# Gate projections of the convolution layer all last, with value pages held in the gate array until then

## Chip, core and metric

One core of a Trainium2 chip runs one launch of the kernel. The time is device microseconds from the launch's first to its last work; the figure given for a kernel is the median of several runs. A separate execution of each kernel is recorded by the hardware profiler.

## What is computed

One step of a two-layer decoder trunk, on a prompt of 1024 positions and on 8 samples of one position each, with shared weights (model width 1024). Layer 0 has stick-breaking attention heads beside causal pooling groups; the samples attend over a paged cache of 4096 past positions. Layer 1 is a convolution module with a gate:

```python
def c_mix(x, conv_prev, w_in, w_dw, b_dw, cn_g, cn_b, w_out):
    p = x @ w_in
    a, a_gate, gate = jnp.split(p, [CONV_WIDTH, 2 * CONV_WIDTH], axis=-1)
    h = a * jax.nn.sigmoid(a_gate)
    h_ext = jnp.concatenate([conv_prev.astype(h.dtype), h], axis=1)
    c = lax.conv_general_dilated(h_ext, w_dw[:, None, :], ..., feature_group_count=CONV_WIDTH)
    c = jax.nn.silu(layer_norm(c + b_dw, cn_g, cn_b))
    return (c * jax.nn.silu(gate)) @ w_out, h_ext[:, -CONV_STATE:]
```

For the samples, layer 0 needs `o = w . v_past`: 8 samples x 32 pages of 128 positions x 512 values, fetched through `page_table`. Those 256 pages of 256 KB are the value pages of this document.

## The kernel before

**The stretch that matters** is the input projection of layer 1 with the convolution, from some 600 us to 970 us of the span. The generator `c_gen` puts out the projection in 48 *slots*. A slot is one block of 128 output features times one half (512 positions) of the prompt: 8 values of k, three matmuls each (high x high, low x high, high x low parts of the split operands, L225 to L227), so 24 matmuls into one of two accumulators `acc`, then an evacuation by ScalarE. Blocks come in the order of the list `blocks`: `ag0, a0, ag1, a1, ...`; `GATE_AFTER = (3,)` puts the first gate block `g0` behind `a3`, and `g1` to `g7` stand behind `a7`. The last two blocks are interleaved, so that the half 0 of `g6` and `g7` precedes the half 1 of either. I write a3/1 for half 1 of block a3.

- `evac_ag` writes the sigmoid of the gate of channel block cb, `evac_a` copies the block and multiplies (GpSimd) into `HBUF[cb]`, of which there are two buffers. Before a new one is written, the block cb - 2 must be through: `evac_a` first puts out all its remaining taps, and the buffer is free once its last tap (VectorE) and `tail_rows` (a TensorE transposition, put out four points after the join) have read it.
- `conv(cb)` puts the 31 taps of the depthwise convolution of one channel block in two lists: `heads` (ScalarE product L1372, GpSimd addition L1375) and `taps` (VectorE, L1383 and L1385, and a closing addition `join`, L1390). `cpoint`, called four times a slot, pops 1.575 heads and 1.46 taps from them.
- `tick(n)` advances the sample work in `queue` by n steps: first `decode_v`, then `sample_path`. A step of `decode_v` loads four value pages (`v_tile` gives the buffers, a ring of `VB = 9`) and multiplies each with four 32-column matmuls side by side (L1163). The main loop gives `VRATE = 1.575` steps a slot, and 2.7 when only `sample_path` is left.
- When the taps of block 7 are through, the statistics are summed (L1422), and `stats_3` queues the normalization `midq`: broadcast rows by transposition (`mid_a`, L1569), subtract and scale (`mid_b`, VectorE, L1581), SiLU (`mid_s`, ScalarE, L1595); `cpoint` pops one entry per call. After the loop, `mid_g` multiplies with the gate, `mid_c` splits the product for the output projection (`out_layer`, L1034 to L1036).
- `G`, the gate array of 32 KB per partition, is written first by `evac_gate(0)`. TensorE, ScalarE, VectorE and GpSimd run in the order in which the code puts instructions out. The order on SyncE, which issues all loads and stores here, is chosen by the framework's planner from its own estimate of when each is ready.

Of the kernel before, what the change touches and what calls it, by code (L numbers as in the profile page):

```python
# [41 lines left out]
NTB = S // P  # L42
# [35 lines left out]
VB = 9  # L78
# [9 lines left out]
FAST = (5, 7)  # L88
WCONVA = ((0, 5), (1, 5))
SY = 2  # L90
VRATE = 1.575
MOM7 = 3
TAPR = 1.46
SHIFT_LAG = 6
MOM_LAG = 6
GATE_AFTER = (3,)
QSCALE = 1.0 / math.sqrt(DH)


# [1 line left out]
def kernel(  # L101
# [33 lines left out]
    def psum(tag, bufs, shape=(P, 512), dt=F32):  # L135
        return (psq[0] if tag == "qv" else ps).tile(list(shape), dt, tag=tag, name=tag, bufs=bufs)
# [9 lines left out]
    def trp():  # L146
        return pz[0].tile([P, 512], F32, tag="zt", name="zt", bufs=NZT[0])
# [203 lines left out]
    def page_ids(b, j, n):  # L351
        _, pg = nc.values_load_multi_w_load_instructions(
            pt[0:1, b * NPG + j:b * NPG + j + n], engines=[SP], min_val=0, max_val=NPOOL - 1,
            skip_runtime_bounds_check_because="page ids index the page pool")
        return pg
# [113 lines left out]
    queue = []  # L469

    def tick(n):
        while n > 0 and queue:
            try:
                next(queue[0])
                n -= 1
            except StopIteration:
                queue.pop(0)
# [414 lines left out]
    t = trp()  # L892
# [54 lines left out]
    for u in range(len(units) + 2):  # L947
# [10 lines left out]
        k = int(tcred)  # L958
# [171 lines left out]
    def fin0(tb, y, h):  # L1130
        sp.dma_start(x1_dram[tb * P:(tb + 1) * P, h], y[:, h])

        def f():
            for hf in range(h.start // 512, h.stop // 512):
# [10 lines left out]
    load_res(1)  # L1145
    out_layer(w_out0, first0, ahead0, X, [gb0], lnp, fin0,
              lambda n4, tb: tick(1), before0, None, tail0, OLAGB, FASTB, WIDE, gps0)
    def v_tile():
        return cd.tile([P, HW], F32, tag="vt", name="vt", bufs=VB)

    def decode_v():
        for hf in range(2):
            Z = W[hf]
            pv = psum("qv", 1)
            for j in range(NPG):
                if j % 2 == 0:
                    pgs = [page_ids(hf * 4 + bi, j, 2) for bi in range(4)]
                vts = []
                for bi in range(4):
                    vts.append(v_tile())  # L1160
                    sp.dma_start(vts[bi], cv[ds(pgs[bi][j % 2], 1)].rearrange("o t f -> t (o f)"))
                for bi in range(4):
                    pe.matmul(pv[32 * bi:32 * bi + 32, :], Z[:, j % 8 * 4 + j // 8, :], vts[bi],  # L1163
                              start=(j == 0), stop=(j == NPG - 1), tile_position=(0, 32 * bi))
                yield
            m = cx.tile([P, HW], F32, tag="pvm", name="pvm", bufs=2)
            act.activation(out=m, in_=pv, func=AF.Copy)
            mh = m.rearrange("p (h d) -> p h d", d=DH)
            gp.tensor_tensor(out=mh, in0=mh, in1=dmask, op=ALU.mult)
            for _ in range(2):  # L1170
                yield
            t = trp()
            for i in range(4):
                pe.matmul(t[:, i * 4:i * 4 + 4], m[:, i * P:(i + 1) * P], selb, start=True, stop=True)
            sh = shs[:, 0:4, hf * 4:hf * 4 + 4]
            act.activation(out=sh, in_=t[:, 0:16].rearrange("p (k b) -> p k b", b=4), func=AF.Copy)
            gp.tensor_tensor(out=sh, in0=sh, in1=sga[:, :, hf * 4:hf * 4 + 4], op=ALU.mult)
# [7 lines left out]
    def issue():  # L1185
        if rows:
            w, f0, k = rows.pop(0)
            ts = []
            for hf in range(2):
                ts.append(v_tile())  # L1190
                sp.dma_start(ts[hf], w[k * P:(k + 1) * P, f0 + hf * HW:f0 + hf * HW + HW])
            issued.append(ts)
# [143 lines left out]
    def evac_a(cb):  # L1336
        def f(c, c0, n, o):
            if c == 0:
                while any(t[0] <= cb - 2 for t in heads):
                    heads.pop(0)[1]()  # L1340
                while any(t[0] <= cb - 2 for t in taps):
                    pop_tap()
                HBUF[cb] = cx.tile([P, KS + S], F32, tag="hbuf", name="hbuf", bufs=2)
                gp.memset(HBUF[cb][:, 0:KS], 0.0)
            hs = HBUF[cb][:, KS + c0:KS + c0 + n]
            act.activation(out=hs, in_=o, func=AF.Copy)
            gp.tensor_tensor(out=hs, in0=hs, in1=CSG[cb][:, c0:c0 + n], op=ALU.mult)
            if c == 1:
                conv(cb)
        return f  # L1350
# [97 lines left out]
    def cpoint():  # L1448
        credit[1] = min(credit[1] + HRATE, 3.0)
        while credit[1] >= 1.0:  # L1450
            credit[1] -= 1.0
            if heads:
                heads.pop(0)[1]()
        credit[0] = min(credit[0] + TAPR, 3.0)
        while credit[0] >= 1.0:
            credit[0] -= 1.0
            if taps:
                pop_tap()
        midpop()

    def evac_gate(g):
        def f(c, c0, n, o):
            act.activation(out=G[:, c0 // P:(c0 + n) // P, g, :], in_=o.rearrange("p (t c) -> p t c", c=P), func=AF.Silu)
        return f

# [2 lines left out]
    def gate_block(g):  # L1468
        blocks.append((w_in1, 2048 + g * P, evac_gate(g), f"g{g}"))

    gn = 0
    for i in range(NK):
        blocks.append((w_in1, 1024 + i * P, evac_ag(i), f"ag{i}"))
        blocks.append((w_in1, i * P, evac_a(i), f"a{i}"))
        if i in GATE_AFTER:
            gate_block(gn)
# [17 lines left out]
    cd = cdp.enter_context(tc.tile_pool(name="cd", bufs=1, reuse_waits="tile"))  # L1494
    C = cd.tile([P, NTB, NK, P], F32, name="conv")
    G = cd.tile([P, NTB, NK, P], F32, name="gate")
    ones32 = cd.tile([P, 32], F32, name="ones32")
    gp.memset(ones32, 1.0)
    onesm = cd.tile([P, P], F32, name="onesm")
# [17 lines left out]
    stats = psum("o", 1)  # L1517

    queue.append(decode_v())
    queue.append(sample_path())  # L1520
    rmu = const.tile([P, 2, 4], F32, name="rmu")
# [75 lines left out]
    def mid_g(c):  # L1597
# [3 lines left out]
        for tb in range(a, b):  # L1601
            (dve if tb in GDVE else gp).tensor_tensor(out=C[:, tb], in0=C[:, tb], in1=G[:, tb], op=ALU.mult)

# [11 lines left out]
    def before(n4, tb):  # L1615
# [8 lines left out]
        if tb == 3:  # L1624
            gb1[0] = G[:, 0:2].rearrange("p t k c -> p t (k c)")
            sp.dma_start(gb1[0][:, 0, :], ln_c_g.to_broadcast([P, D]))
# [7 lines left out]
    vcred = 0.0  # L1634
    while (f"g{NK - 1}", 0) not in fill.seen:
        for i in range(3):
            fill.part()
            cpoint()
        fill.part()
        vcred += VRATE if len(queue) > 1 else 2.7  # L1640
        tick(int(vcred))
        vcred -= int(vcred)
        cpoint()
# [59 lines left out]
```

## Time and profile before

| | us |
|---|---|
| median of 3 runs | 1110.16 (1109.91 to 1115.74) |
| the profiled execution, whole | 1110.31 |
| its span, first to last instruction | 1108.5 |
| TensorE busy / VectorE busy | 1042.0 / 833.3 |
| mean granted TensorE clock | 0.972 |

The profile has a page (busy shares, the span in slices, the costliest groups) and answers questions on the trace: busy time by stretch, instructions of one engine in order of time with what ended the idle time before each, and waits by pair. In the rows of an engine in order of time the first column is the start, the second the duration of the group, both in us; `x8` is the number of instructions in the group, and a bracket gives the idle time before it and what ended that.

### The profile page before, as it was taken

The numbers are of one execution on the slowest core, as the hardware profiler recorded it, in microseconds if no ns is written. First come the engines' busy times: TensorE is split into PE (matmuls) and PEld (weight loads), VectorE is DVE, ScalarE is ACT, GpSimd is POOL, SyncE is SP. The second block draws the span as 40 slices with busy tenths as digits, with TensorE's granted clock in tenths as the row PEclk, the third lists the DMA queues.
The fourth block names the chain that finished last, engine by engine and source line by source line (L and its number), as shares of the span: only waits on it lengthen the run. The fifth ranks groups of instructions, "written<-read, shape, count | busy, mean of one in ns | idle before, by whom it ended". The sixth has DMA issues, their size and how long they took to land.

```text
span 1108.5 us, 19858 instructions
## 1 busy us (share of the span) xinstructions
PE 1042.0 (94%) x6804; PEld 840.1 (76%) x6804; DVE 833.3 (75%) x982; ACT 493.4 (45%) x933; POOL 632.2 (57%) x488
## 2 busy tenths in 40 slices
PE   8899998999999989979988999999999899799996
PEld 7897887888888878979986666566666466678786
DVE  3368899899689988698874699999999960584246
ACT  5245665665766647601143244534543412462111
POOL 3266858567276878568765266757764612342135
PEclk9999999999999989989988999999999999889998
DMA  8577857865457776478425786877687678386933
GB/s 268 171 205 228 253 181 214 257 207 176 131 158 230 243 217 217 151 263 267 155 100 177 218 262 214 267 241 232 208 263 235 205 244 266 111 271 217 321 108 135
DMA packets 179350, 235.20 MB, mean 212 GB/s; under 512 B 15434, under 2 KB 95955, under 8 KB 179225
## 3 DMA queue, kind: packets, MB, share of 16 engines
q1 hardware_dynamic: 179249, 233.94, 67.0%
q8 instruction: 53, 0.87, 0.3%
q14 instruction: 48, 0.39, 0.1%
HBM read 212.60 MB, written 16.14 MB: 206 GB/s over the span
## 4 chain that ended last, share of the span: by engine, by line
PE 51%; POOL 7%; DVE 6%; DMA 5%; issue 2%; ACT 2%; SPq 2%; POOLq 0%; DVEq 0%; ACTq 0%
PE acc L225 10%; PE acc L227 9%; PE acc L226 9%; PE qv L1163 6%; DMA kt<-in_cache_k_dram 3%; POOL kt L417 2%; PE acc L1034 2%; PE acc L1036 2%; PE acc L1035 2%; DVE conv L1581 2%; PE zt L1034 1%; POOL wlo L210 1%; DVE xl L196 1%; PE qv L1199 1%; PE zt L1035 1%
## 5 line engine op out<-in xcount | busy, mean ns | idle before, releaser
L225 PE MATMUL acc<-xh,whi 128*128 128x384 f32 (+2 forms) x960 | 360.3, 375 | 1.9 <-DVE hbt L705 1.4
L227 PE MATMUL acc<-xl,whi 128*128 128x384 f32 (+2 forms) x960 | 339.3, 353 | 0.5 <-DVE xl L196 0.5
L226 PE MATMUL acc<-xh,wlo 128*128 128x384 f32 (+2 forms) x960 | 338.8, 353 | 0.0
L417 POOL TENSOR_TENSOR kt<-kt,qbs 128x1024 f32<-128x1024 f32 x96 | 237.8, 2487 | 79.0 <-DMA kt<-in_cache_k_dram 58.8
L210 POOL TENSOR_TENSOR wlo<-wraw,whi 128x512 fp32r<-128x512 f32 x122 | 163.6, 1345 | 176.6 <-ACT whi L205 154.0
L1385 DVE SCALAR_TENSOR_TENSOR conv_acc<-hbuf,wdwT,conv_acc 128x1024 f32<-128x1024 f32 x196 | 252.8, 1290 | 6.8
L225 PEld LDWEIGHTS acc<-xh,whi 128*128 128x128 f32 x960 | 183.0, 191 | 68.5 <-issue 27.2
L227 PEld LDWEIGHTS acc<-xl,whi 128*128 128x128 f32 x960 | 182.8, 190 | 18.4 <-DVE xl L196 0.9
L226 PEld LDWEIGHTS acc<-xh,wlo 128*128 128x128 f32 x960 | 183.4, 191 | 15.8
L409 DVE TENSOR_REDUCE zw<-kt 128x16 f32<-128x1024 f32 x128 | 152.9, 1211 | 28.0 <-POOL kt L417 23.0
L1375 POOL TENSOR_TENSOR conv<-conv,tap 128x512 f32<-128x512 f32 x84 | 105.9, 1293 | 15.5 <-ACT tap L1372 15.5
L205 ACT ACTIVATE whi<-wraw 128x512 fp32r<-128x512 f32 x126 | 77.6, 625 | 71.9 <-DMA wraw<-in_w_out_ab_dram 55.8
L1034 PE MATMUL acc<-whi,xh 128*128 128x256 f32 x352 | 103.9, 295 | 0.0
L1036 PE MATMUL acc<-whi,xl 128*128 128x256 f32 x352 | 101.0, 287 | 2.2 <-DVE xl L196 2.2
L1035 PE MATMUL acc<-wlo,xh 128*128 128x256 f32 x352 | 100.9, 287 | 0.6 <-POOL wlo L210 0.6
L365 DVE TENSOR_TENSOR_SCAN kp<-kp,zt 128x512 f32<-128x512 f32 (+3 forms) x96 | 92.5, 964 | 6.1 <-ACT zt L361 6.1
L1372 ACT ACTIVATE tap<-hbuf,wdwT 128x512 f32<-128x512 f32 x84 | 59.8, 721 | 46.1 <-POOL conv L1375 37.7
L1163 PE MATMUL qv<-vt,zw 128*32 128x512 f32 x512 | 74.5, 603 | 3.1 <-DMA vt<-in_cache_v_dram 3.1
L360 ACT ACTIVATE kp<-zt,nbiash 128x512 f32<-128x512 f32 (+3 forms) x96 | 55.8, 581 | 46.0 <-PE zt L823 24.5
L1034 PEld LDWEIGHTS acc<-whi,xh 128*128 128x128 f32 x352 | 68.5, 194 | 8.3 <-issue 7.8
L1036 PEld LDWEIGHTS acc<-whi,xl 128*128 128x128 f32 x352 | 68.5, 195 | 2.4 <-DVE xl L196 2.4
L1035 PEld LDWEIGHTS acc<-wlo,xh 128*128 128x128 f32 x352 | 68.5, 195 | 1.1 <-POOL wlo L210 1.0
(286 smaller groups left out, 1501.7 us busy)
## 6 DMA issues: line engine op xcount, KB each, us to landing
kt<-in_cache_k_dram SPq DMA_DIRECT2D x256, 256.0 KB
vt<-in_cache_v_dram SPq DMA_DIRECT2D x256, 256.0 KB
wraw<-in_w_in_c_dram SPq DMA_DIRECT2D x48, 256.0 KB
vt<-in_w_in_c_dram SPq DMA_DIRECT2D x48, 256.0 KB
wraw<-in_w_in_ab_dram SPq DMA_DIRECT2D x46, 256.0 KB
xt<-in_x_prompt_dram SPq DMA_DIRECT2D x8, 512.0 KB
wraw<-in_w_out_ab_dram SPq DMA_DIRECT2D x16, 256.0 KB
xres<-in_x_prompt_dram SPq DMA_DIRECT2D x8, 512.0 KB
```

Source lines behind the costliest of these rows:

```text
L210: (eng or gp).tensor_tensor(out=lo, in0=raw, in1=hi.bitcast(F32), op=ALU.subtract)
L225: pe.matmul(o, hi[:, k % 4, :], xh, start=(k == 0), stop=False)
L226: pe.matmul(o, lo[:, k % 4, :], xh, start=False, stop=False)
L227: pe.matmul(o, hi[:, k % 4, :], xl, start=False, stop=(k == NK - 1))
L409: dve.tensor_reduce(out=seg[:, j // 8, j % 8:j % 8 + 2, bi * 8:bi * 8 + 8], in_=kts.pop(s - KLAG - 1).rearrange("p a (h d) -> p a h d", d=DH),
L417: eng.tensor_tensor(out=kt, in0=kt, in1=qrow[b], op=ALU.mult)
L1034: pe.matmul(o, XH[:, k, cs], hi[:, k % 2, :], start=(k == 0), stop=False)
L1035: pe.matmul(o, XH[:, k, cs], lo[:, k % 2, :], start=False, stop=False)
L1036: pe.matmul(o, XL[:, k, cs], hi[:, k % 2, :], start=False, stop=(k == NK - 1))
L1163: pe.matmul(pv[32 * bi:32 * bi + 32, :], Z[:, j % 8 * 4 + j // 8, :], vts[bi], start=(j == 0), stop=(j == NPG - 1), tile_position=(0, 32 * ...
L1375: gp.tensor_tensor(out=ch, in0=ch, in1=tcs(t), op=ALU.add)
L1385: dve.scalar_tensor_tensor(out=part[1], in0=hb[:, j:j + S], scalar=w, in1=part[1], op0=ALU.mult, op1=ALU.add)
```

## The change

Three things change together. The gate block `g0` goes from behind `a3` to the head of the other gate blocks behind `a7`. Until the first evacuation of a gate block, `v_tile` draws on 16 views of `G` (2 KB per partition each) beside the ring of 9: of 25 buffers handed out in turn, 16 lie in `G`. While that holds, a step of `decode_v` takes eight pages instead of four, and the loop gives half as many steps; the rate is 1.66 instead of 1.575 (times four pages, in both phases).

```diff
-VRATE = 1.575
+VRATE = 1.66
-GATE_AFTER = (3,)
+GATE_AFTER = ()
+    gfree, gturn = [], [0]
+
     def v_tile():
+        gturn[0] += 1
+        if gfree and gturn[0] % (VB + 16) < 16:
+            return gfree[gturn[0] % (VB + 16)]
         return cd.tile([P, HW], F32, tag="vt", name="vt", bufs=VB)
...
-                yield
+                if j % 2 or not gfree:
+                    yield
...
     def evac_gate(g):
         def f(c, c0, n, o):
+            gfree.clear()
             act.activation(out=G[:, c0 // P:(c0 + n) // P, g, :], in_=..., func=AF.Silu)
...
     G = cd.tile([P, NTB, NK, P], F32, name="gate")
+    gfree.extend(G[:, t, i * 4:i * 4 + 4, :].rearrange("p k c -> p (k c)") for t in range(NTB) for i in range(2))
...
-        vcred += VRATE if len(queue) > 1 else 2.7
+        vcred += (VRATE / 2 if gfree else VRATE) if len(queue) > 1 else 2.7
```

## Rows read from the trace of the kernel before

**Rows 1.** The page, engines: busy time, share of the span, instructions.
```profile
PE 1042.0 (94%) x6804; PEld 840.1 (76%) x6804; DVE 833.3 (75%) x982; ACT 493.4 (45%) x933; POOL 632.2 (57%) x488
```

**Rows 2.** Busy time by stretch: length, then PE, PEld, DVE, ACT, POOL (instructions), clock, DMA.
```profile
635.00:650.00 15.00, 15.00 (x76) 9.94 (x75) 14.58 (x13) 3.55 (x6) 3.44 (x3) 1.00 0.83 260
...
905.00:920.00 15.00, 15.00 (x77) 9.89 (x76) 0.00 (x0) 2.23 (x4) 2.58 (x2) 1.00 0.82 247
```

**Rows 3.** TensorE in order of time, around two interruptions by value pages.
```profile
610.33 0.40 PE L227 MATMUL acc<-xl,whi 128*128 128x512 f32 x1
...
611.99 0.39 PE L226 MATMUL acc<-xh,wlo 128*128 128x512 f32 x1
...
617.11 0.40 PE L227 MATMUL acc<-xl,whi 128*128 128x512 f32 x1
617.43 1.92 PE L1163 MATMUL qv<-vt,zw 128*32 128x512 f32 x16
...
619.63 0.40 PE L226 MATMUL acc<-xh,wlo 128*128 128x512 f32 x1
```

**Rows 4.** TensorE in order of time: value pages that came late.
```profile
701.61 2.63 PE L1163 MATMUL qv<-vt,zw 128*32 128x512 f32 x16
...
709.95 3.67 PE L1163 MATMUL qv<-vt,zw 128*32 128x512 f32 x16
...
863.27 1.90 PE L1163 MATMUL qv<-vt,zw 128*32 128x512 f32 x10
...
872.51 0.53 PE L225 MATMUL acc<-xh,whi 128*128 128x512 f32 x1
```

**Rows 5.** The chain that ended last: one summing of the statistics.
```profile
719.41 0.99 PE o L1422 x8
```

**Rows 6.** ScalarE in order of time: evacuations of a0/1, a7/0, a7/1, a wait, g7/0.
```profile
617.54 0.60 ACT L1346 ACTIVATE hbuf<-acc 128x512 f32<-128x512 f32 x1 [5.14 <-PE acc L227]
...
846.34 0.60 ACT L1346 ACTIVATE hbuf<-acc 128x512 f32<-128x512 f32 x1 [9.51 <-PE zt L1394]
...
847.76 0.60 ACT L1346 ACTIVATE hbuf<-acc 128x512 f32<-128x512 f32 x1 [0.16 <-PE acc L227]
...
858.37 1.34 ACT L1372 ACTIVATE tap<-hbuf,wdwT 128x512 f32<-128x512 f32 x2 [7.32 <-DMA out_dram<-hst]
...
948.07 0.58 ACT L1463 ACTIVATE gate<-acc 128x512 f32<-128x512 f32 x1
```

**Rows 7.** VectorE in order of time: taps of blocks 4 and 5, last join.
```profile
767.33 31.77 DVE L1385 SCALAR_TENSOR_TENSOR conv_acc<-hbuf,wdwT,conv_acc 128x1024 f32<-128x1024 f32 x24
...
801.85 31.77 DVE L1385 SCALAR_TENSOR_TENSOR conv_acc<-hbuf,wdwT,conv_acc 128x1024 f32<-128x1024 f32 x24
...
902.77 1.23 DVE L1390 TENSOR_TENSOR conv<-conv_acc,conv 128x1024 f32<-128x1024 f32 x1
```

**Rows 8.** SyncE's queue in order of time: eight value pages issued.
```profile
796.21 6.42 SPq L1161 DMA_DIRECT2D vt<-in_cache_v_dram  x8
```

**Rows 9.** SyncE's waits from 590 to 950 us: total us, times, longest.
```profile
SPq L1161 <- PE qv L1163: 56.8, 39, 10.9
```

**Rows 10.** VectorE in order of time: the normalization (L1581).
```profile
944.00 2.48 DVE L1581 TENSOR_TENSOR conv<-conv,rows 128x1024 f32<-128x1024 f32 x2 [5.08 <-PE rows L1570]
...
965.39 14.40 DVE L1581 TENSOR_TENSOR conv<-conv,zt 128x1024 f32<-128x1024 f32 x12
```

**Rows 11.** TensorE in order of time, after the loop.
```profile
957.58 0.45 PE L1569 MATMUL zt<-ident,rmu 128*128 128x128 f32 x1 [5.24 <-DVE conv L1581]
...
968.69 0.28 PE L1034 MATMUL acc<-whi,xh 128*128 128x256 f32 x1
...
982.12 0.58 PE L1036 MATMUL acc<-whi,xl 128*128 128x256 f32 x1 [2.22 <-DVE xl L196]
```

**Rows 12.** Busy time by stretch after the loop, columns as in Rows 2.
```profile
954.00:962.00 8.00, 4.42 (x16) 3.92 (x17) 4.19 (x4) 4.22 (x10) 1.27 (x1) 0.57 0.37 133
...
982.00:989.00 7.00, 6.88 (x35) 5.85 (x36) 4.72 (x10) 5.51 (x12) 4.96 (x3) 0.52 0.97 333
```

## Prediction

> **What bounds the kernel now.** I read the busy shares first: TensorE is busy 94% of the span and VectorE 75% [rows 1]. Both are averages, so I went on to the table of busy time by stretch. In the convolution stretch TensorE is full and VectorE works 14.58 of 15 us; between 905 and 920 us VectorE does nothing while TensorE stays full [rows 2]. So there are two chains in this stretch: TensorE's 48 slots, and VectorE's taps, which run without a gap to the last join at 902.77 [rows 7]. They meet in `HBUF`: block cb can't be evacuated before the taps of cb - 2 are through.
>
> TensorE's chain can be added up. A slot is 24 matmuls; undisturbed matmuls start 0.233 us apart (611.99 to 617.11 is 22 of them), so 5.59 us. A step of four pages costs 610.33 to 611.99 less two such spacings, 1.19 us; eight pages in one place cost 617.11 to 619.63 less two, 2.05 us [rows 3]. A summing of the statistics costs 0.99 us [rows 5]. Counting what `cpoint` and `tick` put out by their credits, a0/1 to a7/1 holds 30 slots, 16 places with eight pages, 13 with four, 5 summings and some 2.7 us of short products: 167.7 + 32.8 + 15.5 + 5.0 + 2.7 = 223.7 us. The evacuations stand 847.76 - 617.54 = 230.2 us apart [rows 6], so TensorE lost 6.5 us there. From a7/1 to g7/0 it is 12 slots, 7 and 4 places, 3 summings and 1.5 us: 90.8 us of work in 100.3 us [rows 6], 9.5 us lost. The losses are late pages (two such places took 0.7 and 1.75 us over the 1.92 of an undisturbed one, one held TensorE from 863.27 to 872.51 [rows 3, 4]) and, at 851 us, ScalarE held 7.32 us by a small store [rows 6].
>
> After the loop the normalization is what ends last: TensorE waits 5.24 us and later 2.22 us for VectorE [rows 11]. After each, the granted clock falls to its lower level (1.2 GHz), and 4.42 us of work at a mean of 0.57 and 6.88 us at 0.52 [rows 12] lose 1.9 and 3.3 us.
>
> **The change part by part.**
>
> *Eight-page steps and 25 buffers.* The count gives 30 places with eight pages and 4 with four, against 23 and 18: 64 groups of four in both, in 34 instead of 41 places. A place less saves 2 x 1.19 - 2.05 = 0.33 us, so 2.3 us in all. SyncE issues eight pages in 6.42 us [rows 8], within the 5.59 + 2.05 = 7.64 us of a slot with such a step, and it now spends 56.8 us waiting for TensorE to free buffers [rows 9]. With 25 buffers most of that wait goes, and I take the 6.5 us lost before a7/1 as gone (bounds 0 to 6.5 us left). What hides the rest is below: here it doesn't matter.
>
> *Gate block g0 goes behind a7.* The 16 slots up to a3 are as before. From a4 on every `a` block comes two slots earlier, while VectorE's taps do not. The first page step now stands behind a0/1, so TensorE ends that at 616.3 and VectorE runs 1.2 us earlier. To the end of a5/1: 20 slots, 16 places, 3 summings and 1.7 us, 765.6 us; the taps of block 3 end before that. To a6/1: 22.4 + 3 x 2.05 (one stands behind a6/1) + 1.0 + 0.9, 796.0 us; the taps of block 4 end at 799.1 - 1.2 = 797.9 [rows 7], plus 0.8 us for the evacuation: TensorE waits until 798.7, **2.7 us**. To a7/1: 22.4 + 6.1 + 1.0, 828.2 us; the taps of block 5 end at 833.6 - 1.2 = 832.4 [rows 7], so g0/0 starts at **833.2**, after 5.0 us. So the pages' gain ahead of a7 turns into a wait for VectorE; in turn up to 7.7 us of late pages there cost nothing.
>
> *From a7 to the statistics.* Before, g1/0 starts at 847.8 with 12 slots to go up to g7/0; now g0/0 starts at 833.2 with 14. In work that is a draw. What differs is the order: the last join stands at the end of g3/1, two slots earlier in the list, and VectorE ends it at 904.0 - 1.2 = 902.8, before TensorE asks for its result (904 to 907 us). `stats_3` then stands inside g5/1 instead of g7/0, and all eleven entries of `midq` are popped within the loop. To there: 11.5 slots 64.3, 8 x 2.05 + 3 x 1.19 = 20.0, summings and row products 3.5: 87.8 us, so the first `mid_b` pass is due at 921.5 us. To this I add 1.9 us for the clock after the 5.0 us wait (as after the 5.24 one [rows 11, 12]) and late pages: the gate evacuation clears the 16 buffers, the ring is 9 again, and four times two eight-page places follow each other, the first pair loaded ahead. SyncE's 6.42 us and the landing barely fit in 7.64; I take the middle of the two late places, 1.2 us, for each of the other three pairs: 3.6 us (bounds 0 and the 9.5 us now lost here). **First pass at 927.0**, against 944.00 [rows 10].
>
> *To the output projection.* Before, 968.69 - 944.00 = 24.7 us from the first pass to its first matmul [rows 10, 11]. Now two more slots and a page step lie in that stretch (+12.4), and the 5.24 us wait with its 1.9 us of clock goes (-7.1). New is that `midq` meets the slots with two transposition buffers: the 16 passes at 1.2 us [rows 10] need 19.2 us, the third group ends some 2.2 us after TensorE wants its buffer for the fifth, and a later one 1.6 us: +3.8. That makes 33.8, the output projection at 960.8; half the price of the other fall of the clock for that wait, 1.7 us (bounds 0 and 3.3), gives **962.5**, 6.2 us earlier.
>
> The Trainium skill, "TensorE: Matmul & The Clock Gate", section "Why this matters for your kernels", warns that a gap between bursts of matmuls puts the array back on half its clock, which speaks against a change that makes gaps. The trace agrees for both waits of rows 11. By that rule, with 3.3 us for the wait at a7 and for the one on `midq`, the sum would be 3.0 us higher.
>
> *Within the output projection* VectorE has its passes behind it, so the 2.22 us wait and its 3.3 us of clock go: 5.5 us. The sample work keeps its place (the last page step stays behind g5/1), and so does everything to the end.
>
> **Sum:** 6.2 + 5.5 = 11.7 us off the profiled execution's 1110.3 us, which is 0.15 us above the median: 1098.6, forecast **1098.5 us**.
>
> **The rivals.**
> - *The losses behind a7 recur in full* (9.5 instead of 3.6 + 1.9 us): the store of `tail_rows(5)` again stands between `hst` and the first heads of block 7, and a7's evacuations, SiLU table and twelve heads bunch on ScalarE. For it: the 7.32 us wait [rows 6]; against: SyncE should be free while TensorE waits at a7. 1102.6 us; if VectorE is then late for the 982 us wait too, 1108.
> - *Slower:* in the slots of the gate blocks, on the ring of 9 at the higher rate, an eight-page place is late as the one at 863.27 was, 9.2 us instead of 2.05 [rows 3, 4], with SyncE stuck behind a weight load. Each costs 7.2 us; from three of the eight on, the kernel is slower by over 0.5%; four give 1098.5 + 28.8 - 3.6 = 1124 us. Against it: this happened once in 23 such places.
> - *The buffers bring no lead,* since SyncE's issue is the limit. Then the 6.5 us before a7 stay and are absorbed by the wait for VectorE: 1098.5 to 1100 us. The Trainium skill, "Perfetto Trace Analysis", section "What 'DMA-bound' means", says that with a solid issuing sequencer larger transfers matter, which would make the buffers idle. The 56.8 us of waits for buffers [rows 9] speak against it.
> - *Nothing is lost behind a7,* neither pages nor clock nor `midq`: 921.5 + 30.0 = 951.5, 17.2 + 5.5 us off, 1087.6 us.
>
> **How the numbers follow.** Forecast 0.48, full losses 0.22, slower 0.15, no lead 0.08, nothing lost 0.07. The range is 1088 to 1110 us: it takes in all but the slower case and the lowest edge. A measurement here tells 0.5% from no change, that is 1104.6 and 1115.7 us. The forecast, the no-lead and the lossless case (0.63) lie below, and of the full losses a fifth (0.04): 0.67 faster; the rest of them same, 0.18; slower 0.15.
>
> **What would show it.** Right: TensorE waits for VectorE's taps through `acc` at some 796 and 828 us, g0/0 starts near 833 us, the last join stays near 903 us, L1581 starts near 927 us and ends inside the loop, the output projection starts near 962 us without a wait of 2 us in its first groups. Wrong: a `hbuf` evacuation of a7 far from 833 us (then VectorE doesn't run as before), page waits over 5 us after 840 us, or L1581 still running in the output projection.

## The result: 0.6% slower

The changed kernel takes **1116.36 us** (median, 1114.09 to 1122.58), the kernel before in the same comparison 1111.53 us (1105.54 to 1115.74); the ratio is 1.006, with a 95% interval of 1.0042 to 1.0078. Forecast was 1098.5 us, so 18 us are missing.

Five events split the span: the evacuations of a0/1 and of a7/0 (ScalarE), the first `mid_b` pass (VectorE), the first matmul of the output projection (L1034), the end. TensorE's instructions up to a0/1 are the same in both kernels but for one step of four pages, which the kernel before takes ahead of it (1.2 us, [rows 3]) and the changed one behind it; yet over the traces of this study a0/1 comes anywhere from 613.1 to 624.1 us, so only what lies behind it is compared. From a0/1 to the end the traces say 491.0 us before and 497.8 after; the difference, 6.8 (5.6 with that step), is near that of the medians, 4.8. The forecast column is worked out from the prediction's times (616.3, 832.4, 927.0, 962.5, and 1108.5 - 11.7 = 1096.8).

| stretch | before | forecast | after | miss |
|---|---|---|---|---|
| a0/1 to a7/0 | 228.8 | 216.1 | 215.7 | -0.4 |
| a7/0 to first `mid_b` | 97.7 | 94.6 | 103.7 | +9.1 |
| to the output projection | 24.7 | 35.5 | 35.0 | -0.5 |
| output projection to the end | 139.8 | 134.3 | 143.3 | +9.0 |

Two stretches came as forecast, two missed by 9 us each. The rows of the changed kernel follow. A *place* is a point between slots at which `tick` takes its steps, a *group* is four value pages (V1.15 is group 15 of the second half of the samples), and SyncE *stands* while its next issue waits for a buffer.

ScalarE in order of time (start, length, line, tiles, in brackets the idle time before it and what ended it): the evacuations of a0/1 and a7/0, the wait for the store, and the weight conversion behind it; they answer to [rows 6].

```profile
621.64 0.60 ACT L1352 ACTIVATE hbuf<-acc 128x512 f32<-128x512 f32 x1 [3.95 <-PE acc L227]
...
837.38 0.60 ACT L1352 ACTIVATE hbuf<-acc 128x512 f32<-128x512 f32 x1 [5.82 <-PE zt L1400]
...
845.95 1.33 ACT L1378 ACTIVATE tap<-hbuf,wdwT 128x512 f32<-128x512 f32 x2 [3.86 <-DMA out_dram<-hst]
...
848.71 0.61 ACT L205 ACTIVATE whi<-wraw 128x512 fp32r<-128x512 f32 x1
```

TensorE in order of time, the places with value pages behind a7 [rows 4]. The first takes its 1.92 us. The second begins at 853.11 and the next slot at 863.06, 9.95 us later; undisturbed that is 1.86 us (845.47 to 847.33). So 8.1 us are lost at one place (the expectations below go by the last matmul's start and call it 9.4 and 7.4). The waits in brackets are 2.2 us of it; in the rest the matmuls start one by one as their pages land, and TensorE counts as busy. Three later places of eight pages take 4.09, 3.77 and 3.19 us (from 883.39, 908.85 and 934.54), so that late pages take some 13.6 us in all.

```profile
845.47 1.92 PE L1168 MATMUL qv<-vt,zw 128*32 128x512 f32 x16
847.33 0.50 PE L225 MATMUL acc<-xh,whi 128*128 128x512 f32 x1
...
853.11 1.05 PE L1168 MATMUL qv<-vt,zw 128*32 128x512 f32 x2
...
856.10 1.05 PE L1168 MATMUL qv<-vt,zw 128*32 128x512 f32 x2 [1.94 <-DMA vt<-in_cache_v_dram]
857.40 5.73 PE L1168 MATMUL qv<-vt,zw 128*32 128x512 f32 x12 [0.26 <-DMA vt<-in_cache_v_dram]
...
863.06 0.50 PE L225 MATMUL acc<-xh,whi 128*128 128x512 f32 x1
```

SyncE's queue in order of time, then its waits from 590 to 950 us and from 835 to 1000 us (total, times, longest) [rows 8, 9]. The two weight loads take 10.13 us, since the second stands until GpSimd has freed a raw buffer; seven of the late place's eight pages are issued only behind it, as TensorE comes to them. Over the stretch, SyncE's wait for value buffers fell from 56.8 to 25.1 us as the buffers were meant to bring about, and its wait for weight buffers stands at 68.5 us, 21.8 of them in seven stands from 835 us on.

```profile
835.17 6.30 SPq L1166 DMA_DIRECT2D vt<-in_cache_v_dram  x8
841.57 0.41 SPq L1403 DMA_DIRECT2D out_dram<-hst  x1
842.09 10.13 SPq L200 DMA_DIRECT2D wraw<-in_w_in_c_dram  x2
853.17 5.93 SPq L1166 DMA_DIRECT2D vt<-in_cache_v_dram  x8
```

```profile
SPq L200 <- POOL wlo L210: 68.5, 17, 11.5
SPq L1166 <- PE qv L1168: 25.1, 24, 3.9
...
SPq L200 <- POOL wlo L210: 21.8, 7, 9.3
```

GpSimd in order of time, and the chain of waits over the same stretch. The store is issued only behind eight pages. GpSimd waits for ScalarE's tap product, which waited for the store; its subtraction L210 at 850.51 frees the raw buffer; the chain then runs through SyncE's issue and the pages' transfer.

```profile
846.75 3.80 POOL L1381 TENSOR_TENSOR conv<-conv,tap 128x512 f32<-128x512 f32 x3 [3.29 <-ACT tap L1378]
850.51 1.29 POOL L210 TENSOR_TENSOR wlo<-wraw,whi 128x512 fp32r<-128x512 f32 x1
```

```profile
853.20 0.34 SPq L1166
...
854.28 3.07 DMA vt<-in_cache_v_dram
```

VectorE: last join and first `mid_b` pass [rows 7, 10]; the join is 3.45 us later than before, less than a0/1 itself (4.1), so VectorE's chain is as forecast.

```profile
906.22 1.23 DVE L1396 TENSOR_TENSOR conv<-conv_acc,conv 128x1024 f32<-128x1024 f32 x1
...
941.10 1.22 DVE L1589 TENSOR_TENSOR conv<-conv,rows 128x1024 f32<-128x1024 f32 x1 [8.47 <-PE rows L1578]
```

TensorE at the start of the output projection [rows 11], then three stretches (length, busy time of PE, PEld, DVE, ACT, POOL, clock, DMA share, GB/s) [rows 12]. The first of them, from 954 us, still lies in the loop: TensorE waits there for VectorE (1.82 us), as forecast, and the clock stays up. The wait of 2.22 us for VectorE is gone. In its place stand waits for weights (1.29 and 0.96) and for the sample path's weight rows (0.46 and 2.12), and two falls of the clock to its lower level, one behind each pair.

```profile
976.14 0.39 PE L1034 MATMUL acc<-whi,xh 128*128 128x256 f32 x1 [1.29 <-ACT whi L205]
977.48 0.58 PE L1035 MATMUL acc<-wlo,xh 128*128 128x256 f32 x1 [0.96 <-POOL wlo L210]
...
988.09 0.63 PE L1205 MATMUL qv<-vt,sB 128*32 128x256 f32 x4 [0.46 <-DMA vt<-in_w_out_ab_dram]
...
991.73 1.74 PE L1205 MATMUL qv<-vt,sB 128*32 128x256 f32 x8 [2.12 <-DMA vt<-in_w_out_ab_dram]
```

```profile
954.00:962.00 8.00, 4.82 (x27) 3.58 (x26) 7.90 (x7) 2.68 (x5) 0.39 (x1) 1.00 0.00 0
977.00:981.00 4.00, 3.52 (x19) 2.49 (x20) 0.00 (x0) 0.71 (x2) 4.00 (x4) 0.57 0.60 205
991.00:998.00 7.00, 6.27 (x30) 4.98 (x31) 1.50 (x3) 3.83 (x6) 2.37 (x1) 0.51 1.05 385
```

ScalarE and SyncE there: twelve SiLU passes of the normalization, popped inside the loop now, stand ahead of the projection's weight conversion; and SyncE stands at weight loads again before it issues the rows.

```profile
969.09 6.00 ACT L1603 ACTIVATE conv<-conv,pvec 128x256 f32<-128x256 f32 x12
...
975.47 1.13 ACT L205 ACTIVATE whi<-wraw 128x512 fp32r<-128x512 f32 x2
```

```profile
977.46 5.17 SPq L200 DMA_DIRECT2D wraw<-in_w_out_c_dram  x3
982.67 0.93 SPq L1197 DMA_DIRECT2D vt<-in_w_out_ab_dram  x2
```

### The profile page after: what moved, and what is told of

Same layout as the page of the kernel before. It is cut to its first block, busy times and chain, and to the rows that moved or that the text cites. A ratio compares the mean times of both kernels' runs of the same rounds, so it can differ in the third digit from the quotient of the medians.

```text
span 1119.4 us, 19844 instructions
## 1 busy us (share of the span) xinstructions
PE 1047.5 (94%) x6804; PEld 844.4 (75%) x6804; DVE 836.1 (75%) x982; ACT 491.5 (44%) x931; POOL 627.5 (56%) x488
## 4 chain that ended last, share of the span: by engine, by line
PE 45%; POOL 9%; DVE 8%; DMA 5%; issue 4%; ACT 2%; SPq 1%; POOLq 0%; DVEq 0%; ACTq 0%
PE acc L225 9%; PE acc L226 8%; PE acc L227 8%; PE qv L1168 5%; POOL kt L417 3%; POOL wlo L210 2%; PE acc L1034 2%; POOL conv L1381 2%; DVE zw L409 1%; PE zt L1034 1%; DMA kt<-in_cache_k_dram 1%; DVE xl L196 1%; PE qv L1205 1%; PE acc L1036 1%; PE acc L1035 1%
## 5 line engine op out<-in xcount | busy, mean ns | idle before, releaser
L210 POOL TENSOR_TENSOR wlo<-wraw,whi 128x512 fp32r<-128x512 f32 x122 | 163.1, 1340 | 184.5 <-ACT whi L205 177.2
L1034 PE MATMUL acc<-whi,xh 128*128 128x256 f32 x352 | 104.8, 298 | 1.3 <-ACT whi L205 1.3
L1034 PEld LDWEIGHTS acc<-whi,xh 128*128 128x128 f32 x352 | 69.4, 197 | 9.9 <-issue 7.0
L369 DVE TENSOR_TENSOR sg<-zt,kp 128x511 f32<-128x511 f32 (+4 forms) x96 | 53.6, 558 | 5.5
```

The costliest lines, as they stand in the source:

```text
L210: (eng or gp).tensor_tensor(out=lo, in0=raw, in1=hi.bitcast(F32), op=ALU.subtract)
L1034: pe.matmul(o, XH[:, k, cs], hi[:, k % 2, :], start=(k == 0), stop=False)
```

## The experiments

All were timed against the kernel before, whose medians lay between 1109.6 and 1111.5 us. The stages are worked out as above, from the same five events of each trace: A to B is a0/1 to a7/0, B to C to the first `mid_b` pass, C to D to the output projection, D to E to the end. Ahead of a0/1 the kernels before, e1, e2 and f2 have taken one group of pages, f3 two and the others none.

| kernel | us | ratio to before (95%) | A to B | B to C | C to D | D to E |
|---|---|---|---|---|---|---|
| before | | 1 | 228.8 | 97.7 | 24.7 | 139.8 |
| after | 1116.4 | 1.0060 (1.0042 to 1.0078) | 215.7 | 103.7 | 35.0 | 143.3 |
| e1_order | 1122.4 | 1.0121 (1.0095 to 1.0147) | 221.8 | 100.6 | 38.4 | 142.2 |
| e2_fours | 1108.4 | 0.9984 (0.9962 to 1.0005) | 222.7 | 97.1 | 34.2 | 133.9 |
| e3_gpq | 1118.8 | 1.0083 (1.0055 to 1.0111) | 220.9 | 101.4 | 35.0 | 142.0 |
| e5_noload | 1103.1 | 0.9935 (0.9914 to 0.9956) | 215.7 | 90.3 | 35.1 | 143.3 |
| f1_held88 | 1103.1 | 0.9938 (0.9915 to 0.9961) | 217.5 | 96.0 | 33.9 | 135.4 |
| f2_fours160 | 1107.6 | 0.9970 (0.9948 to 0.9992) | 215.2 | 95.1 | 35.0 | 141.8 |
| f3_held110 | 1115.7 | 1.0035 (1.0017 to 1.0053) | 231.3 | 92.5 | 34.3 | 135.1 |
| f4_before166 | 1126.9 | 1.0127 (1.0104 to 1.0149) | | | | |
| g1_ticks5 | 1112.3 | 1.0023 (0.9997 to 1.0049) | 215.5 | 102.4 | 40.3 | 131.4 |
| g2_cap | 1115.7 | 1.0051 (1.0024 to 1.0078) | 215.6 | 102.5 | 35.2 | 142.3 |
| g3_both | 1111.9 | 1.0016 (0.9992 to 1.0041) | 215.9 | 102.4 | 40.3 | 134.3 |
| h1_early | 1111.1 | 1.0015 (0.9990 to 1.0040) | 215.5 | 98.2 | 35.1 | 142.9 |
| h2_oneq | 1117.1 | 1.0061 (1.0038 to 1.0083) | 215.5 | 103.4 | 35.0 | 144.0 |
| g4_half | 1098.3 | 0.9895 (0.9860 to 0.9929) | 220.4 | 91.8 | 33.9 | 137.8 |

### The parts of the change, one at a time

**e1_order**, the gate order alone on the kernel before:

```
-GATE_AFTER = (3,)
+GATE_AFTER = ()
```

> The kernel before with the gate blocks moved last and nothing else: ring of nine pages throughout, steps of four pages, the old rate. Theory (A): VectorE's taps set when a7's first half leaves (about 836 us) with or without held pages, because TensorE has slack there; behind a7 the pages are late as in the changed kernel. Then 1115 to 1119 us, within 0.3% of the changed kernel. Rival (B): the held pages are what makes the early part fast; without them the waits for pages before a7 (6.5 us or more) come on top: 1121 to 1125. Rival (C): the gate order alone is a gain and the held pages' end is what costs: under 1108.

1.2% slower than before: rival B. The order alone costs 11.8 us, and buffers, steps and rate together win 6 of them back. The place behind a7 is late here too, 9.9 us (857.05 to 866.99). TensorE in order of time:

```profile
857.05 1.90 PE L1163 MATMUL qv<-vt,zw 128*32 128x512 f32 x10
863.12 3.87 PE L1163 MATMUL qv<-vt,zw 128*32 128x512 f32 x6 [4.16 <-DMA vt<-in_cache_v_dram]
```

**f4_before166**, the rate alone on the kernel before (`VRATE = 1.66`):

> The kernel before with its rate at 1.66 and nothing else of the change: 49 instead of 46 groups ahead of a7's second half, 7 instead of 1 steps of the sample path ahead of the loop's end. Theory (P): the output projection gets shorter by 6 to 9 us, the waits for pages before a7 grow by up to 5: 1103 to 1108. Rival (R): nine buffers can't feed a higher rate, the page waits grow by as much as the projection gains: 1110 to 1114.

Neither: 1126.9 us, 1.3% slower. Its traced execution had a mean granted clock of 0.678, the others 0.966 to 0.979, so only the time is read; where it loses was not seen.

**e2_fours**, the changed kernel with steps of four pages:

```
-                if j % 2 or not gfree:
-                    yield
+                yield
...
-        vcred += (VRATE / 2 if gfree else VRATE) if len(queue) > 1 else 2.7
+        vcred += VRATE if len(queue) > 1 else 2.7
```

> The changed kernel with steps of four pages while the gate array is held (rate not halved). Theory (A): the longer TensorE time of the four-page steps (1.19 us twice against 2.05 us once, some 20 times: about 7 us) lies beside VectorE's taps, so a7's first half leaves within 2 us of 836 us and the time is 1114 to 1119. Rival (B): the steps of eight carry the early gain: 1120 to 1124. Rival (C): steps of eight leave SyncE in a bad phase when the held pages end: under 1112.

In time rival C: 8 us faster than the changed kernel. The early stretch gets 7.0 us longer, but 6.6 us come back behind a7 and 9.4 in the output projection. So both misses shrink by an edit that is in neither stretch. Most of the early loss reads as the store's chain, here ahead of a7: SyncE issues fourteen pages before the store, ScalarE stands for it, and TensorE waits 6.1 us in all for ScalarE's evacuations of the sigmoid blocks (`csg`), where the changed kernel waits 0.85. SyncE, ScalarE and TensorE in order of time:

```profile
802.64 12.33 SPq L1166 DMA_DIRECT2D gate<-in_cache_v_dram  x14
...
818.71 1.33 ACT L1377 ACTIVATE tap<-hbuf,wdwT 128x512 f32<-128x512 f32 x2 [13.36 <-DMA out_dram<-hst]
...
823.30 0.50 PE L225 MATMUL acc<-xh,whi 128*128 128x512 f32 x1 [3.81 <-ACT csg L1338]
```

### Is it the steps, or where they put the work?

By the order of the program, e2 has 46 groups of four pages ahead of a7's second half where the changed kernel has 44, and 7 steps of the sample path ahead of the loop's end where that has 2. The half rate also halves the steps that hold no pages (two behind the first half of the pages). **f1_held88** gives the eight-page steps that position, **f2_fours160** takes it from the four-page ones:

```
-        vcred += (VRATE / 2 if gfree else VRATE) if len(queue) > 1 else 2.7
+        vcred += (0.88 if gfree else VRATE) if len(queue) > 1 else 2.7
```

> The changed kernel, eight-page steps as they are, with a credit of 0.88 in place of 0.83 per place while the gate array is held. By the order of the program this puts 46 instead of 44 groups of pages ahead of a7's second half, the last page in g4/1 instead of g5/1, and 7 instead of 2 steps of the sample path ahead of the loop's end: the same places as the kernel with steps of four. Theory (P, the place in the queue): what the kernel with steps of four gained over the changed one is that its pages and sample products come earlier; then this one is as fast, 1106 to 1110. Rival (S, the steps): eight-page steps themselves cost it; then no gain, 1114 to 1118.

> Steps of four pages with the gate array held, at a rate of 1.6 in place of 1.66: 44 groups ahead of a7's second half, the last page in g5/1 and 2 steps of the sample path ahead of the loop's end, as in the changed kernel. Theory (P): it loses what steps of four at 1.66 gained, 1114 to 1119. Rival (S): steps of four are good at either rate, 1106 to 1110.

f1 goes with the place in the queue, at 1103.1 us even below its range; steps of eight are not what costs. f2 was expected to be slow by the same theory and is not. Its stages tell why: the output projection is long, as in every kernel of the new gate order with 1 or 2 steps of the sample path ahead (141.8 to 144.0 us), and short in every one with 7 or more (131.4 to 137.8 us); but behind a7 it is fast. It also is as fast as the changed kernel up to a7 (215.2 us), so steps of four alone don't bring e2's 7.0 us there; nor do two more groups alone, for f1 has them and is 1.8 us longer. ScalarE's longest stand for the store there is 13.36 us in e2, 10.04 in f1, 6.86 in f2 and 8.68 in the changed kernel; what makes it longest in e2 was not tested. Behind a7 and in the projection there are two causes, and only the one in the output projection goes with the sample path's position.

**f3_held110** takes the same edit further (1.1):

> The changed kernel with a credit of 1.1 in place of 0.83 per place while the gate array is held: 58 groups ahead of a7's second half (44 before), 29 steps of the sample path ahead of the loop's end (2 before). Theory (P): the 14 groups moved ahead of a7 take TensorE some 14 us, of which its 3.5 us of waits there hide a part, and what follows a7 loses them and all late pages; the sample products moved out of the output projection cost the same wherever they stand unless VectorE's passes hide them: 1096 to 1104. Rival (T): pages can't be transferred at this rate (58 groups of 1 MB in some 225 us), TensorE waits for them before a7: over 1108.

1115.7: the time is rival T's, the mechanism in part. Moving 14 groups ahead of a7 makes that stretch 15.6 us longer, the next 11.2 us shorter and the projection 8.2, and the median shows little of the gain (0.7 us). The waits for pages ahead of a7 are few (the largest 1.01 us), but a place of sixteen pages ends 10.2 us after its start at 678.94, where an undisturbed one (765.47 to 769.04) takes 3.57: there the pages were late. The rest is the groups' own time. The last pages of that place, TensorE:

```profile
688.15 1.05 PE L1168 MATMUL qv<-gate,zw 128*32 128x512 f32 x2 [1.01 <-DMA gate<-in_cache_v_dram]
```

### What the loads behind a7 cost, and who makes them late

**e5_noload** leaves out the loads of the last 18 groups (their matmuls read old pages):

> The changed kernel without the loads of the last 18 groups of four value pages (their matmuls read the pages of group 45 again, so part of the decode attention is left out). It prices everything that page loads cost behind a7. Theory (A): of the 12 us by which the changed kernel misses what the early part gained, 10 to 12 are the late pages behind a7 and the clock falls that follow them: 1103 to 1107. Rival (B): most of the loss lies in the output projection and has other causes (late weights, sample rows): 1110 to 1115.

Theory A. B to C falls to 90.3 us: the loads cost the changed kernel 13.4 us there, clock included, and it reaches 1103.1. The output projection stays at 143.3, so the miss there doesn't hang on the one behind a7.

**e3_gpq** takes SyncE's stands away by loading the convolution stage's weights from GpSimd's queue (`wq[0]` is `sp` or `gp`):

```
-        sp.dma_start(raw, src.rearrange("(k p) f -> p k f", p=P))
+        wq[0].dma_start(raw, src.rearrange("(k p) f -> p k f", p=P))
...
+    wq[0] = gp
     while (f"g{NK - 1}", 0) not in fill.seen:
...
+    wq[0] = sp
```

> The changed kernel with the weight loads of the convolution stage issued from GpSimd's queue, so that SyncE never stands at a weight buffer. Theory (A): SyncE's stand of 10.1 us at the weight loads behind a7 is what made the pages late there (9.4 us for a place of 2.05 us, and three smaller ones). With it gone the late pages behind a7 shrink from about 11 us to 4 us or less and the clock falls less: 1106 to 1111. Rival (B): the pages are late because nine buffers and the transfers are too slow, whoever issues: 1114 to 1118. Rival (C): issuing on GpSimd delays the weight conversion, which TensorE then waits for: over 1118.

Rival C, though TensorE's wait is not the one that it names. SyncE's wait for weight buffers is gone, its wait for value buffers is large again (95.5 us), and the late place behind a7 needs 4.07 us; B to C is 2.3 us shorter. But A to B is 5.2 us longer: two loads are issued at 669.01 behind GpSimd's own work, ScalarE's weight conversion waits for them, and VectorE for the ScalarE instruction behind that. VectorE's taps stay that much later, TensorE waits for them three times (8.7 us), at a7/1 4.43 us, and the clock is at its lower level from 838 to 843 us (0.50). ScalarE and VectorE in order of time, one of SyncE's waits from 590 to 950 us, and TensorE in order of time:

```profile
673.45 0.63 ACT L207 ACTIVATE whi<-wraw 128x512 fp32r<-128x512 f32 x1 [5.28 <-DMA wraw<-in_w_in_c_dram]
...
675.57 2.08 DVE L1416 TENSOR_TENSOR conv<-conv,m 128x1024 f32<-128x1024 f32 x1 [4.82 <-ACT m L1412]
```

```profile
SPq L202 <- POOL wlo L212: 2.9, 2, 2.1
```

```profile
838.86 0.79 PE L227 MATMUL acc<-xh,whi 128*128 128x512 f32 x1 [4.43 <-ACT hbuf L1354]
...
855.58 4.07 PE L1170 MATMUL qv<-vt,zw 128*32 128x512 f32 x16
```

The Trainium skill, "DMA: Bandwidth & Descriptors", section "Issuing engines are not separate DMA queues", says that issuing on several engines saves only the issuing sequencer's time. Here it moved a wait as well: 68.5 us of SyncE's standing at weight buffers became 2.9.

**g2_cap** moves V1.15 from the late place to the next (one group instead of two at that place):

```
...
-        tick(int(vcred))
-        vcred -= int(vcred)
+        n = min(int(vcred), 1) if place == 31 else int(vcred)
+        place += 1
+        tick(n)
+        vcred -= n
```

> The changed kernel with one group of pages (V1.15) moved from the place behind g0/1 to the next place, so that no two places of eight pages stand next to each other right after the held pages end. SyncE's stand at the weight loads there stays. Theory (L): the place that took 9.4 us for eight pages had to wait since its pages could be issued only after that stand; with four pages fewer there the loss of 7.4 us shrinks to 3 or less: 1110 to 1114. Rival (M): the wait only moves to the next place: 1115 to 1118.

Rival M: 1115.7 us, B to C 102.5. Half the pages, and still one by one:

```profile
844.68 1.04 PE L1168 MATMUL qv<-vt,zw 128*32 128x512 f32 x2
...
847.62 1.05 PE L1168 MATMUL qv<-vt,zw 128*32 128x512 f32 x2 [1.89 <-DMA vt<-in_cache_v_dram]
```

**h2_oneq** gives GpSimd only the two loads that SyncE stood at, those of block g2 (`wq[0] = gp if bi == 18 else sp` in `fetch`); **h1_early** leaves the stand and takes the step V1.12, V1.13 one place earlier, behind a7/1, which was empty because the half rate had no credit there, and where the gate array's space is still to be had:

```
...
+        n = {29: 1, 30: 0}.get(place, int(vcred))
         vcred -= int(vcred)
+        place += 1
+        tick(n)
```

> The changed kernel with the two weight loads of block g2 alone issued from GpSimd's queue. Theory (L, the stand): SyncE is free from 842 us on and issues V1.14 and V1.15 when the ring's buffers come free (846 to 848 us), so that the place behind g0/1 loses 2 us or less in place of 7.4: from a7's first half to the first mid_b pass 95 to 98 us, and 1108 to 1112 in all. Rival: a later stand, at the weights of g3 or g4, or the ring of nine itself makes them as late: 1114 to 1118.

> The changed kernel with one step of eight pages (V1.12 and V1.13) taken at the empty place behind a7/1, in the gate array's space, instead of behind g0/0; everything from V1.14 on stands where it stood. Theory (E, the empty place): the ring's nine pages are then V1.14 and V1.15, loaded before SyncE's stand at the weights of g2, and the loss of 7.4 us goes: from a7's first half to the first mid_b pass 95 to 97 us in place of 103.7, and 1108 to 1111 in all. Rival: the loss only moves to V1.16 to V1.18 behind the next stand: 1114 to 1118.

In h2 the place behind g0/1 is nearly whole (3.52 us), and the loss comes back two places on (861.57 to 870.05, 8.5 us for 1.92), behind a load of weights that SyncE issues at 861.65 only; the time is that of the changed kernel, as the rival has it. TensorE and SyncE in order of time:

```profile
844.59 3.52 PE L1172 MATMUL qv<-vt,zw 128*32 128x512 f32 x16
...
861.57 1.90 PE L1172 MATMUL qv<-vt,zw 128*32 128x512 f32 x10
865.91 4.14 PE L1172 MATMUL qv<-vt,zw 128*32 128x512 f32 x6 [2.44 <-DMA vt<-in_cache_v_dram]
```

```profile
861.65 0.39 SPq L202 DMA_DIRECT2D wraw<-in_w_in_c_dram  x1
```

In h1 SyncE stands even longer at the weights, 14.73 us, and the eight-page place during it takes its 1.92 us, because its pages were in the ring. The next place, of four pages, takes 4.6 us where one of f2 takes 1.06. B to C is 98.2 us (95 to 97 expected) and the kernel 1111.1, the upper edge of what was expected. SyncE and TensorE in order of time:

```profile
837.03 14.73 SPq L200 DMA_DIRECT2D wraw<-in_w_in_c_dram  x3
```

```profile
846.83 1.92 PE L1168 MATMUL qv<-vt,zw 128*32 128x512 f32 x16
...
854.47 3.30 PE L1168 MATMUL qv<-vt,zw 128*32 128x512 f32 x6
```

So it is neither one stand nor the size of a place. A stand costs what TensorE wants during it beyond the pages that are already loaded, and nine buffers hold little more than one eight-page place. By the program's order f1 and f2 stand like h1: the place behind a7/1 takes its pages from the gate array's space, and the ring holds the next ones when the stand comes; both are fast behind a7.

### The output projection

**g1_ticks5** takes five more steps of the sample path ahead of the projection (`tick(5)` behind the main loop); **g3_both** adds g2's edit:

> The changed kernel with five more steps of the sample path taken between the last gate block and the output projection (7 instead of 2 ahead of it, as in the kernel with the credit of 0.88). Theory (O): the output projection took 143.3 us in the changed kernel and 135.4 in that one because the first sample product stands inside it, with its weight rows late; moved ahead it costs at most its own 5 to 6 us there, under VectorE's passes less: 1108 to 1113. Rival (N): the steps cost the same at either place: 1115 to 1118.

> Both of these edits together in the changed kernel. If the late place behind g0 and the sample steps inside the output projection are the two things that cost it, the gains add and it reaches the kernel with the credit of 0.88 (1103): 1101 to 1107. If there is only one cause that shows at two places, it is no faster than the better of the two alone: 1108 to 1113.

g1: theory O, 1112.3 us. The projection falls by 11.9 us, the stretch before it grows by 5.3; of these 6.6 us the medians show 4.1. Most of the products moved run in one piece, without a wait for their rows:

```profile
956.95 3.64 PE L1205 MATMUL qv<-vt,sB 128*32 128x256 f32 x32 [1.38 <-POOL sB L1261]
```

g3 (1111.9) is no better than g1, as g2 had brought nothing.

### A version that beats both

Each gate block writes one eighth of the gate array, so half of the held space is free until g4. **g4_half** is f1 with the space given back in two halves:

```
...
-            gfree.clear()
+            if g in (0, 4) and c == 0:
+                gfree[:] = gfree[8:] if g == 0 else []
...
```

> The kernel with the credit of 0.88, and the gate array given back in two halves: the first gate block takes eight of the sixteen held pages' space, the fifth the other eight, so that the ring holds 17 pages, not 9, from g0 to g4. Theory (L): SyncE can run ahead of its stands at weight loads, the late pages behind a7 (5 to 6 us against the kernel without those loads) go: 1097 to 1101. Rival (M): SyncE's stands themselves limit when pages are issued, whatever the ring holds: 1102 to 1105.

**1098.3 us**, 1% faster than the kernel before. Theory L. B to C is 91.8 us, 1.5 above the kernel without those loads (which has one group more to multiply there, about 1 us). SyncE issues seven pages into the gate array's space behind a pair of weight loads that takes 3.30 us here:

```profile
847.70 3.30 SPq L200 DMA_DIRECT2D wraw<-in_w_in_c_dram  x2
851.19 5.54 SPq L1167 DMA_DIRECT2D gate<-in_cache_v_dram  x7
```

## Why the prediction was wrong, point by point

- **Eight-page steps and 25 buffers: right.** No page is late between a0/1 and a7, and SyncE's wait for value buffers falls from 56.8 to 25.1 us. The rival without lead is out. That the lead is worth something only as far as VectorE lets it was right as well: 215.7 us against 216.1. e1, without the buffers, is 6.1 us longer there; f2, with buffers and steps of four, is not, so the buffers bring it and not the steps.
- **The waits for VectorE at a6/1 and a7/1 (2.7 and 5.0 us): right in sum, not in form.** a7/0's evacuation comes when VectorE is through with block 5, as forecast (its join starts at 837.18). But TensorE shows no wait for taps: its lead was gone before, in part by waits of 0.85, 0.75 and 1.93 us for ScalarE and GpSimd and by the clock, at a mean of 0.64 from 826 to 830 us. The longest wait is for a late weight conversion, and ahead of that stands the chain that is found again behind a7: ScalarE's taps had waited 8.68 us for the store, until 815.75. The sum had none of these losses; that the stretch agrees rests on VectorE alone. Where VectorE is later, in e3, 4.43 us appear at the place named. TensorE:

```profile
826.61 0.50 PE L226 MATMUL acc<-xh,wlo 128*128 128x512 f32 x1 [1.93 <-POOL wlo L210]
```

- **From a7 to the statistics: the step that failed.** The work itself was sized rightly: without the page loads the stretch takes 90.3 us, and the forecast less its 3.6 us of late pages was 91.0. The term for late pages was 3.6 us with an upper bound of 9.5, and is 13.4 with the clock: place by place 8.1 at the pair that the sum put at nothing and 5.5 at the other three. Two sentences in it were wrong. "The first pair loaded ahead" held for the first place only: by 853 us one page of the second was issued. And the test of "6.42 us within 7.64" compared SyncE's issue with TensorE's time as if SyncE did nothing else; what it does besides is stand at weight loads. The row was there: in the kernel before, the view that gave 56.8 us for value buffers says next

```profile
SPq L200 <- POOL wlo L210: 29.9, 14, 7.3
```

  and the sum did not follow it, though a rival did. As the wait for value buffers went, that one grew to 68.5 us. (The sum also slips by 0.5 us: 833.2 and 87.8 make 921.0, not 921.5.)
- **The rival "losses behind a7 recur in full" was the right one there,** though short of the 13.4 us, and had the cause: the store stands behind SyncE's pages, ScalarE's taps wait 3.86 us for it, GpSimd waits for these, the weight conversion comes late, and SyncE waits for that. That the store begins the chain is read from the rows; no run moves the store. The "slower" rival had the mechanism too (SyncE behind a weight load, 7.2 us a place; measured 8.1), but asked for three such places. One, with smaller ones, was enough, because the next step failed as well.
- **First pass to output projection: right,** 35.0 for 35.5, with the two waits for `midq` as forecast (1.82 and 1.36 us for 2.2 and 1.6). That the number fits so well is in part luck: 1.7 us of it were for a fall of the clock that did not come, and the wait of 1.29 us for the projection's weights, which the sum doesn't have, lies at the end of this stretch.
- **Within the output projection: wrong by 9.0.** The 2.22 us wait for VectorE did go. But the passes that are now early bring SiLU passes ahead of the projection's weight conversion (2.25 us of waits), the sample rows come late behind SyncE's weight loads (2.58 us), and the clock falls twice where it fell once [rows 12]. Estimated from these rows, without the 1.29 us ahead of the first matmul: waits 3.5 us in place of 2.5 (2.22 and a small one of 0.27), and of the clock 4.0 x 0.43 + 7.0 x 0.49 = 5.1 us in place of 7.0 x 0.48 = 3.4; that is 2.7 us longer than before, where 3.5 are measured, and the 5.5 us that the forecast took off make up the rest. "The sample work keeps its place" was true, and was itself a cost: kernels that put its first product ahead of the projection are 6 to 12 us shorter there. How those divide between the products' own time, late rows and the clock was not separated.
- **The clock.** The prediction gave half the price of a fall to the wait on `midq`. The clock stayed at 1.00 there, and fell behind the waits of 1.29 and 0.96 us on weights. The Trainium skill, "TensorE: Matmul & The Clock Gate", section "Why this matters for your kernels", has gaps between bursts of matmuls put the array back on half its clock; the trace agrees for the waits on weights and not for those on `midq`.

What stays open: why the kernel before at a rate of 1.66 is 1.3% slower, what makes ScalarE's stand for the store longest in e2, and what a store that doesn't wait behind SyncE's pages would bring.

## What to carry to other kernels

An in-order issuing queue that serves two kinds of buffers has to be read with all its waits: when the larger one is taken away, ask which one it meets next, and who frees that. Moving the loads to another engine's queue puts them behind that engine's own work. A lead that is given back at a point must be judged at that point, by what is loaded when the queue next stands; here eight pages taken one place earlier were worth 5 us, and giving the space back in halves 5 us to f1. And work that is put out by a credit per place lands elsewhere after any change of the rate: its position in every later stage belongs in the sum.

## What was not expected of the hardware

- Executions of the same TensorE instructions differ by up to 11 us at a0/1 (613.1 us in e5, 624.1 in f1), with falls of the granted clock at differing times ahead of it (from 587 to 593 us it was 0.50 in e5 and 1.00 in f1, from 598 to 604 the other way round). Counted from a0/1, eleven of the fourteen kernels with a trace stand to the kernel before as their medians do, within 2 us; f3, g1 and g4 miss by 2.7, 4.0 and 4.2 us, so a stage's difference of less than that is not to be leaned on.
- An eight-page place whose pages land one by one shows TensorE as busy: of the 8.1 us lost at 853 us the waits in brackets are 2.2. The list of waits alone would have hidden the largest piece.
